# One hybrid decoder step on one core: scaled tokens transposed, vector rows in the token pool, stored decode rows written from SBUF

## The chip, the cores and the metric

The kernel runs on one core of one Trainium2 chip. The metric is the device time of one execution in microseconds. Engines are named PE (TensorE, matrix products), DVE (VectorE), ACT (ScalarE), POOL (GpSimd) and SP (SyncE, which issues most DMAs).

## The reference, cut to what matters

Two layers, each a token mixer and a squared-ReLU MLP. The first mixer is a causal Conformer convolution, the second RWKV-7 time mixing. There is one prompt of 1024 tokens with 16 learned meta tokens ahead of it, and eight decode sequences with one new token each.

```python
def _rmsnorm(x, g):
    y = xf * lax.rsqrt(jnp.mean(xf * xf, axis=-1, keepdims=True) + RMS_EPS)
    return (y * g).astype(x.dtype)

def _conformer_conv(h, buf, w_pw1, b_pw1, w_dw, b_dw, ln_g, ln_b, w_pw2, b_pw2):
    u = h @ w_pw1 + b_pw1
    u = u[..., :D_MODEL] * jax.nn.sigmoid(u[..., D_MODEL:])
    full = jnp.concatenate([buf, u], axis=1)             # buf: 30 stored rows of a sequence
    c = lax.conv_general_dilated(full, w_dw[:, None, :], ...)   # 31 taps, one filter per channel
    ...                                                  # LayerNorm over the channels -> cn
    out = jax.nn.silu(cn) @ w_pw2 + b_pw2
    return out, full[:, -CONV_BUF:]                      # the new 30 rows

for i in range(DEPTH):                                   # DEPTH = 2, D_MODEL = 1024, D_FF = 4096
    hn = _rmsnorm(h, norm_mix[i])
    out, ... = conformer_conv(hn, ...) if i == 0 else rwkv7(hn, ...)
    h = h + out
    h = h + square(relu(_rmsnorm(h, norm_mlp[i]) @ w_mlp_in[i])) @ w_mlp_out[i]
```

All data is float32. For a decode sequence the new conv state is its stored rows 1 to 29 and the new row; `conv_sample` (8, 30, 1024) is an output, and so are the prompt's last 30 rows, the RWKV states and the final norm of the tokens.

## The kernel before, in words

**Dense products.** The 1048 tokens are worked in three groups of 352, 348 and 348 columns (G0; the eight decode tokens are the last columns of group 2). Activations lie with the channel on the partition, so the tokens are transposed once, at the start. Each float32 operand is split into a high and a low part, and a product is the sum of three matmuls (`mm3`, L187 to L189): high by high, low weight by high, high weight by low. One weight tile is 1024 x 128 (512 KB), 24 matmuls. SP loads it into a slot of the pool "raw" (`load_raw`, L146; five slots), ACT casts the high part (L157), POOL subtracts the low part (L162), and both stand in a ring of slots until PE has used them.

**Who orders the work.** The program is written as generators: the main line (dense products) calls `fill()`, which lets a background generator go on for some points. On top of that the framework simulates a timeline and gives each engine its own fixed order of instructions; an engine carries out its list in that order and waits by semaphores, so an instruction that waits holds up all that stands behind it on its engine. DMA issues stand in these lists too. The issues of SP and ACT go round over eight completion counters, and a counter's next user waits until its last one has landed.

**The beginning** (`transpose_x`, `load_x`, `load_vecs`, `load_dw`). For each group, up to 128 tokens at a time land in `xt` (L414). ACT squares and sums them (L417; the squares go to a throwaway tile `xj`), takes the root (L418), DVE inverts it (L419): this is the factor of the RMS norm, in `ss[:, 2:3]`. PE transposes the raw tokens into `tx` (L450) for the residual. For the normed tokens DVE builds the diagonal matrix `dg` of the factors (L462) and PE multiplies `xt` with it (`tn`, L466): this transposes and scales in one float32 matmul. ACT (L468) and DVE (L469) then multiply by the norm's gain and split into `hn_h` and `hn_l`. Meanwhile `load_vecs` gathers the small vectors as rows of `stg` and transposes them, and `load_dw` does so with the convolution's 31 x 1024 weights (`wst`, L437; `ptw`, L440; `wdw`, L441). Both staging tiles are slots of the raw weight pool.

**The first mixer.** `pw1` makes `u` from the two halves of the first pointwise product (`pg`, `pa`; sigmoid at L481, product at L483). `conv` runs the 31 taps on DVE (L501, L504). The prompt's groups follow one another in the background of the dense products; `mean_parts` gathers the means of the LayerNorm (`acc_mu`, L223), which PE sums at L231.

**The decode rows.** `conv_states` writes the new rows (`cst`, `csd`; L545, L546). `conv_dec` loads the stored rows of eight sequences, in two tiles of 4 x 30 rows (`sdec`, L515), transposes them by channel block (`pw`, L521), copies them beside the new token's column (`win`, L523, L524) and sums the taps. `cst`, `csd` and the two `sdec` tiles share two slots. The stored rows 1 to 29 also go to the output `conv_sample`, by eight copies from DRAM to DRAM on ACT's queue (L1573). They stand late in the program's text, but have no input of the kernel's own to wait for, and the order puts them at 0.8 to 20.4 us.

After the first MLP comes the RWKV layer: its projections, 17 chunks of recurrence between them and the second MLP, the decode step and the final norm.

Of the kernel before, what the change touches and what calls it, by code (L numbers as in the profile page):

```python
# [8 lines left out]
F32 = mybir.dt.float32  # L9
F32R = mybir.dt.float32r  # L10
BF16 = mybir.dt.bfloat16
AF = mybir.ActivationFunctionType
ALU = mybir.AluOpType
# [3 lines left out]
P = 128  # L17
D = 1024
# [4 lines left out]
DEC = 8  # L23
NP_TOK = META + SEQ
T = NP_TOK + DEC
CW = 31
CB = CW - 1
# [21 lines left out]
def hybrid_step(tc, x_prompt, x_sample, state_conv, state_shift, state_wkv, meta_tokens,  # L49
# [8 lines left out]
    nc = tc.nc  # L58
    ctx = ExitStack()
    with ctx:  # L60
# [4 lines left out]
        ident = consts.tile([P, P], F32, name="ident")  # L65
# [3 lines left out]
        eps_t = consts.tile([P, 4], F32, name="eps_t")  # L69
        for i, e in enumerate((RMS_EPS, LN_EPS, GN_EPS)):  # L70
            nc.vector.memset(eps_t[:, i:i + 1], e)

        dram = pool(ctx, "dram", 1, space=bass.MemoryType.DRAM)
        d_x2 = dram.tile([P, KT, G0[2][1]], F32, name="d_x2")
# [47 lines left out]
        cur = {}  # L122
# [6 lines left out]
        def stat(name, tag, bufs, w=None):  # L129
            return cur["stat"].tile([P, w or cur["n"]], F32, name=name, tag=tag, bufs=bufs)  # L130
# [238 lines left out]
        with ExitStack() as l0:  # L369
# [36 lines left out]
                    out.append((c, w, parts))  # L406
                return out

            def load_x(pl, g):
                tiles = []  # L410
                for i, (c, w, parts) in enumerate(segments(g)):
                    xt = pl.tile([P, D], F32, name=f"xt{g}_{i}", tag="xt")
                    for r0, src in parts:
                        nc.sync.dma_start(xt[r0:r0 + src.shape[0], :], src)  # L414
                    junk = pl.tile([P, D], BF16, name=f"xj{g}_{i}", tag="xj", bufs=1)
                    ss = stat(f"ss{g}_{i}", "ss", 4, 4)
                    nc.scalar.activation(junk[:w, :], xt[:w, :], AF.Square, accum_out=ss[:w, 0:1])  # L417
                    nc.scalar.activation(ss[:w, 1:2], ss[:w, 0:1], AF.Sqrt, scale=1.0 / D, bias=eps_t[:w, 0:1])  # L418
                    nc.vector.reciprocal(ss[:w, 2:3], ss[:w, 1:2])  # L419
                    tiles.append((c, w, xt, ss))  # L420
                return tiles

            def load_vecs(tiles):

                for i in tiles:
                    st = cur["raw"].tile([P, D], F32, name=f"stg{i}", tag="raw")[:, :P]
                    nc.gpsimd.memset(st, 0.0)
                    for q, (name, ap) in enumerate(v for v in vecs if col[v[0]] // P == i):
                        r = col[name] % P
                        (nc.gpsimd if q % 2 else nc.scalar).dma_start(st[r:r + ap.shape[0], :], ap)  # L430
                    pt = bank("ptp")
                    nc.tensor.transpose(pt[:, :P], st, ident)
                    nc.vector.tensor_copy(pvec[:, i * P:(i + 1) * P], pt[:, :P])

            def load_dw():
                wst = cur["raw"].tile([P, D], F32, name="wst", tag="raw")[:CW, :]
                nc.scalar.dma_start(wst, conv_w_dw.rearrange("l w c -> (l w) c"))  # L437
                pt = bank("ptw")
                for k in range(KT):
                    nc.tensor.transpose(pt[:, k * CW:(k + 1) * CW], wst[:, k * P:(k + 1) * P], ident[:CW, :CW])  # L440
                nc.vector.tensor_copy(wdw, pt[:, :KT * CW].rearrange("p (k w) -> p k w", k=KT))  # L441

            def transpose_x(g, ah, al):
                n = G0[g][1]
                tiles = load_x(xin, g)
                yield 4
                for k in range(KT):
                    ps = bank(f"tx{g}_{k}")
                    for c, w, xt, ss in tiles:
                        nc.tensor.transpose(ps[:, c:c + w], xt[:w, k * P:(k + 1) * P], ident[:w, :w])  # L450
                    if g < 2:
                        (nc.scalar.copy if g else nc.vector.tensor_copy)(h[g][:, k, :n], ps[:, :n])
                    else:
                        t = tt(f"xs{k}", "t1")
                        nc.scalar.copy(t[:, :n], ps[:, :n])
                        nc.sync.dma_start(d_x2[:, k, :], t[:, :n])
                    yield 1
                if g == 0:
                    load_vecs([0])
                dg = stat(f"dg{g}", "acc0", 1)  # L460
                for c, w, xt, ss in tiles:
                    nc.vector.tensor_scalar(dg[:w, c:c + w], ident[:w, :w], ss[:w, 2:3], None, op0=ALU.mult)  # L462
                for k in range(KT):
                    ps = bank(f"tn{g}_{k}")
                    for c, w, xt, ss in tiles:
                        nc.tensor.matmul(ps[:, c:c + w], xt[:w, k * P:(k + 1) * P], dg[:w, c:c + w], start=True, stop=True)  # L466
                    gk = vec("norm_mix", k)
                    nc.scalar.activation(ah[:, k, :n], ps[:, :n], AF.Copy, scale=gk)  # L468
                    nc.vector.scalar_tensor_tensor(al[:, k, :n], ps[:, :n], gk, ah[:, k, :n].bitcast(F32),  # L469
                                                   op0=ALU.mult, op1=ALU.subtract)  # L470
                    yield 1
# [39 lines left out]
            def conv_dec(c, c_col):  # L511

                sd = [decp.tile([P, D], F32, name=f"sdec{i}", tag="st", bufs=2)[:4 * CB, :] for i in range(2)]
                for i in range(2):
                    nc.sync.dma_start(sd[i], state_conv[0, 4 * i:4 * i + 4].rearrange("b w d -> (b w) d"))  # L515
                yield 1
                for m in range(KT):
                    win = decp.tile([P, DEC, CW], F32, name=f"win{m}", tag="win")
                    ps = bank(f"pw{m}", "x")
                    for i in range(2):  # L520
                        nc.tensor.transpose(ps[:, i * 4 * CB:(i + 1) * 4 * CB], sd[i][:, m * P:(m + 1) * P],  # L521
                                            ident[:4 * CB, :4 * CB])
                    nc.scalar.copy(win[:, :, :CB], ps[:, :DEC * CB].rearrange("p (b w) -> p b w", b=DEC))  # L523
                    nc.gpsimd.tensor_copy(win[:, :, CB:CW], udec[:, m, :].unsqueeze(2))  # L524
                    nc.vector.tensor_mul(win, win, wdw[:, m:m + 1, :].broadcast_to([P, DEC, CW]))
                    rd = decp.tile([P, DEC], F32, name=f"rd{m}", tag="rd")
                    nc.vector.tensor_reduce(rd, win, axis=AX.X, op=ALU.add)
                    nc.scalar.activation(c[:, m, c_col:c_col + DEC], rd, AF.Identity, bias=vec("b_dw", m))
                    yield 1
# [935 lines left out]
        with ExitStack() as l1:  # L1465
# [103 lines left out]
            mixer_out(1, residp2, actp, fill, add)  # L1569
            for _ in rest:  # L1570
                pass
            for q in range(DEC):
                nc.scalar.dma_start(o_conv_sample[0, q, 0:CB - 1, :], state_conv[0, q, 1:CB, :])  # L1573
            g1 = group(1, actp, hidp, sums)
            fill, rest = filler(2 * KT + MLP2_POINTS, ([ranked(FN, final(0))], FB))
            add, sums = sums_of(2)
# [43 lines left out]
```

## Time and profile before

| what | value |
|---|---|
| runs | 2867.08, 2878.38 and 9711.41 us; median 2878.38 |
| profiled execution, time | 2870.67 us |
| its span in the profile | 2869.0 us |
| granted PE clock | 0.961 |
| busy share of PE, DVE, ACT, POOL | 94%, 68%, 47%, 59% |
| DMA traffic | 428.34 MB, 149 GB/s over the span |

A busy share is an average over stages with different limits, so the profile is read stage by stage: windows give the busy time of each engine in a stretch, and the timeline lists instructions with their start, length, engine and line, and in brackets the idle time before them and what ended it. Times are from the span's start. One of the three runs took more than three times as long as the others; the median is taken as it stands.

### The profile page before, as it was taken

To read this page: it belongs to the slowest core of one execution; us is meant where nothing else is said; L and a number is where in the kernel's file an instruction comes from. 1 tells how busy PE (TensorE), PEld (TensorE's weight loads), DVE (VectorE), ACT (ScalarE), POOL (GpSimd) and SP (SyncE) were. 2 spreads that over 40 slices of the span, in tenths; PEclk is the share of its full clock that TensorE was granted. 3 is DMA by queue.
4 is the path that set the end of the run, shared out by engine and by line. 5 is a ranking of instruction groups with operands and counts; after the bars stand their busy time and mean duration, and the time that the engine had idled before them with its cause. 6 is when DMAs were issued, how large, how long until landed. Compare 5 with 4: busy or idle time off the path is not lost. (4 is left out here: it accounts for less than half of the span.)

```text
span 2869.0 us, 54486 instructions
## 1 busy us (share of the span) xinstructions
PE 2690.9 (94%) x20554; PEld 2567.2 (89%) x20554; DVE 1962.3 (68%) x3794; ACT 1350.6 (47%) x2515; POOL 1703.3 (59%) x2295
## 2 busy tenths in 40 slices
PE   8999999999999898878799889889999999999998
PEld 8998999999999898867678788778889999999998
DVE  5999999995455546377986885689656764443444
ACT  5545444544354334464666766634445552222223
POOL 6677877887788775444433463656438783433432
PEclk9999999999999999888999999989989999999999
DMA  6662544454444542676788877766556742222211
GB/s 176 178 187 88 155 134 133 138 177 136 140 130 142 175 140 89 201 208 178 200 210 217 236 188 184 204 175 161 134 150 206 205 136 85 67 74 67 67 60 41
DMA packets 659285, 428.34 MB, mean 149 GB/s; under 512 B 126840, under 2 KB 609208, under 8 KB 659022
## 3 DMA queue, kind: packets, MB, share of 16 engines
q1 hardware_dynamic: 652780, 421.93, 52.4%
q10 hardware_dynamic: 6018, 2.89, 0.4%
q8 instruction: 162, 2.65, 0.4%
q14 instruction: 101, 0.83, 0.1%
q0 software_dynamic: 224, 0.03, 0.0%
HBM read 353.03 MB, written 72.66 MB: 148 GB/s over the span
## 5 line engine op out<-in xcount | busy, mean ns | idle before, releaser
L162 POOL TENSOR_TENSOR wo_lo<-wo_raw,wo_hi 128x256 fp32r<-128x256 f32 x736 | 564.1, 800 | 281.8 <-ACT wo_hi L157 269.0
L162 POOL TENSOR_TENSOR wi_lo<-wi_raw,wi_hi 128x256 fp32r<-128x256 f32 x640 | 491.5, 800 | 278.4 <-ACT wi_hi L157 266.3
L187 PE MATMUL out<-hh,wo_hi 128*128 128x352 f32 (+2 forms) x1536 | 504.0, 328 | 20.1 <-DVE h L340 10.9
L340 DVE TENSOR_TENSOR h<-h,out 128x352 f32<-128x352 f32 (+2 forms) x768 | 385.8, 509 | 196.8 <-PE out L189 196.2
L187 PE MATMUL ps_in<-m_h,wi_hi 128*128 128x352 f32 (+2 forms) x1536 | 498.3, 325 | 10.3 <-ACT m_h L269 8.3
L188 PE MATMUL out<-hh,wo_lo 128*128 128x352 f32 (+2 forms) x1536 | 499.5, 325 | 0.0
L189 PE MATMUL out<-hl,wo_hi 128*128 128x352 f32 (+2 forms) x1536 | 495.5, 325 | 4.2 <-DVE hl L141 4.2
L188 PE MATMUL ps_in<-m_h,wi_lo 128*128 128x352 f32 (+2 forms) x1536 | 497.2, 324 | 0.0
L189 PE MATMUL ps_in<-m_l,wi_hi 128*128 128x352 f32 (+2 forms) x1536 | 496.2, 323 | 0.0
L504 DVE SCALAR_TENSOR_TENSOR cv<-u,wdw,cv 128x352 f32<-128x352 f32 (+2 forms) x720 | 376.5, 572 | 0.7
L157 ACT CAST wi_hi<-wi_raw 128x1024 fp32r<-128x1024 f32 x160 | 168.1, 1050 | 392.9 <-PE out L189 187.6
L157 ACT CAST wo_hi<-wo_raw 128x1024 fp32r<-128x1024 f32 x184 | 192.9, 1049 | 313.8 <-PE out L189 146.6
L187 PEld LDWEIGHTS out<-hh,wo_hi 128*128 128x128 f32 x1536 | 292.8, 191 | 27.5 <-DVE h L340 14.8
L187 PEld LDWEIGHTS ps_in<-m_h,wi_hi 128*128 128x128 f32 x1536 | 290.6, 189 | 13.6 <-ACT m_h L269 8.4
L189 PEld LDWEIGHTS out<-hl,wo_hi 128*128 128x128 f32 x1536 | 291.9, 191 | 6.5 <-DVE hl L141 5.5
L188 PEld LDWEIGHTS out<-hh,wo_lo 128*128 128x128 f32 x1536 | 292.8, 191 | 1.6
L188 PEld LDWEIGHTS ps_in<-m_h,wi_lo 128*128 128x128 f32 x1536 | 290.7, 189 | 2.0
L189 PEld LDWEIGHTS ps_in<-m_l,wi_hi 128*128 128x128 f32 x1536 | 290.2, 189 | 1.5
L327 DVE SCALAR_TENSOR_TENSOR r<-ps_in,rs_m 128x352 f32<-128x352 f32 (+2 forms) x192 | 98.6, 515 | 234.1 <-PE ps_in L189 230.5
L141 DVE TENSOR_TENSOR hl<-s,hh 128x352 fp32r<-128x352 f32 (+2 forms) x192 | 144.4, 753 | 111.8 <-ACT hh L140 111.6
L329 ACT ACTIVATE s<-r 128x352 f32<-128x352 f32 (+2 forms) x192 | 93.8, 490 | 134.6 <-DVE r L327 134.4
L162 POOL TENSOR_TENSOR wv_lo<-wv_raw,wv_hi 128x256 fp32r<-128x256 f32 x96 | 79.9, 864 | 25.9 <-ACT wv_hi L157 25.6
(403 smaller groups left out, 6195.0 us busy)
## 6 DMA issues: line engine op xcount, KB each, us to landing
wi_raw<-in_w_mlp_in_dram SPq DMA_DIRECT2D x160, 512.0 KB, 4.1
wo_raw<-in_w_mlp_out_dram SPq DMA_DIRECT2D x160, 512.0 KB, 3.7
wr_raw<-in_rwkv_w_r_dram SPq DMA_DIRECT2D x32, 512.0 KB, 6.0
wk_raw<-in_rwkv_w_k_dram SPq DMA_DIRECT2D x32, 512.0 KB, 5.6
wv_raw<-in_rwkv_w_v_dram SPq DMA_DIRECT2D x32, 512.0 KB, 5.4
d_ab<-ab SPq DMA_DIRECT2D x32, 512.0 KB, 3.3
pg_raw<-in_conv_w_pw_dram SPq DMA_DIRECT2D x24, 512.0 KB, 5.1
pa_raw<-in_conv_w_pw_dram SPq DMA_DIRECT2D x24, 512.0 KB, 4.5
```

Of the source, the lines that this page charges most:

```text
L141: eng_lo.tensor_sub(lo, src, hi.bitcast(F32))
L157: nc.scalar.copy(hi[:, :a * b], raw[:, :a * b])
L162: eng_lo.tensor_sub(lo[:, cs], raw[:, cs], hi[:, cs].bitcast(F32))
L187: nc.tensor.matmul(ps, w[0], act[0], start=first, stop=False)
L188: nc.tensor.matmul(ps, w[1], act[0], start=False, stop=False)
L189: nc.tensor.matmul(ps, w[0], act[1], start=False, stop=last)
L327: nc.vector.scalar_tensor_tensor(r[:, :n], ps[:, :n], 0.0, rs[:, :n], op0=ALU.max, op1=ALU.mult)
L329: nc.scalar.activation(s[:, :n], r[:, :n], AF.Square)
L340: nc.vector.tensor_add(hv[:, 4 * i + m, :], hv[:, 4 * i + m, :], ps[:, :n])
L504: nc.vector.scalar_tensor_tensor(acc[m][:, :n], ug[:, m, j:j + n], wdw[:, m, j:j + 1], acc[m][:, :n], op0=ALU.mult, op1=ALU.add)
```

## The change

Four edits, all shown here:

1. The Square's output is kept as a float32 tile (`xn`), which is then overwritten with the scaled tokens (`xt` times the factor; DVE in group 0, ACT in groups 1 and 2). PE transposes it with the identity, in place of the product with a diagonal. The diagonal is gone.
2. One activation with Sqrt stands at the start, on the constants, so that the table of functions is loaded there.
3. `stg` and `wst` are tiles of the token pool `xin`: `stg` has a slot of its own, `wst` is one more user of the three slots of `xn`. The raw pool's five slots hold weights alone.
4. The eight copies from DRAM to DRAM on ACT's queue are gone. In `conv_dec` SP writes rows 1 to 29 of each sequence from the loaded tiles in SBUF.

```diff
         for i, e in enumerate((RMS_EPS, LN_EPS, GN_EPS)):
             nc.vector.memset(eps_t[:, i:i + 1], e)
+
+        nc.scalar.activation(eps_t[:, 3:4], eps_t[:, 0:1], AF.Sqrt)
...
-            def load_x(pl, g):
+            def load_x(pl, g, xns):
...
-                    junk = pl.tile([P, D], BF16, name=f"xj{g}_{i}", tag="xj", bufs=1)
+                    junk = pl.tile([P, D], F32, name=f"xn{g}_{i}", tag="xn")
+                    xns.append(junk)
...
-                    st = cur["raw"].tile([P, D], F32, name=f"stg{i}", tag="raw")[:, :P]
+                    st = xin.tile([P, P], F32, name=f"stg{i}", tag="stg", bufs=1)
...
-                wst = cur["raw"].tile([P, D], F32, name="wst", tag="raw")[:CW, :]
+                wst = xin.tile([P, D], F32, name="wst", tag="xn")[:CW, :]
                 nc.scalar.dma_start(wst, conv_w_dw.rearrange("l w c -> (l w) c"))
...
-                tiles = load_x(xin, g)
+                xns = []
+                tiles = load_x(xin, g, xns)
+                scaled = []
+                for i, (c, w, xt, ss) in enumerate(tiles):
+                    xs = xns[i]
+                    if g:
+                        nc.scalar.activation(xs[:w, :], xt[:w, :], AF.Copy, scale=ss[:w, 2:3])
+                    else:
+                        nc.vector.tensor_scalar(xs[:w, :], xt[:w, :], ss[:w, 2:3], None, op0=ALU.mult)
+                    scaled.append(xs)
                 yield 4
...
-                dg = stat(f"dg{g}", "acc0", 1)
-                for c, w, xt, ss in tiles:
-                    nc.vector.tensor_scalar(dg[:w, c:c + w], ident[:w, :w], ss[:w, 2:3], None, op0=ALU.mult)
                 for k in range(KT):
                     ps = bank(f"tn{g}_{k}")
-                    for c, w, xt, ss in tiles:
-                        nc.tensor.matmul(ps[:, c:c + w], xt[:w, k * P:(k + 1) * P], dg[:w, c:c + w], start=True, stop=True)
+                    for (c, w, xt, ss), xs in zip(tiles, scaled):
+                        nc.tensor.transpose(ps[:, c:c + w], xs[:w, k * P:(k + 1) * P], ident[:w, :w])
...
                 for i in range(2):
                     nc.sync.dma_start(sd[i], state_conv[0, 4 * i:4 * i + 4].rearrange("b w d -> (b w) d"))
                 yield 1
+                for i in range(2):
+                    for q in range(4):
+                        nc.sync.dma_start(o_conv_sample[0, 4 * i + q, 0:CB - 1, :], sd[i][q * CB + 1:(q + 1) * CB, :])
+                    yield 0
...
-            for q in range(DEC):
-                nc.scalar.dma_start(o_conv_sample[0, q, 0:CB - 1, :], state_conv[0, q, 1:CB, :])
```

## The prediction

> **What bounds the kernel now.** I read the page first, for the engine that fills the span and for the chain of waits that ended last.
>
> ```profile
> span 2869.0 us, 54486 instructions
> PE 2690.9 (94%) x20554; PEld 2567.2 (89%) x20554; DVE 1962.3 (68%) x3794; ACT 1350.6 (47%) x2515; POOL 1703.3 (59%) x2295
> PE   8999999999999898878799889889999999999998
> ## 4 chain that ended last, share of the span: by engine, by line
> PE 27%; POOL 5%; DVE 5%; issue 3%; DMA 2%; ACT 1%; SPq 0%; DVEq 0%; POOLq 0%; ACTq 0%
> ```
>
> TensorE (PE) is busy for 2690.9 of 2869.0 us, which leaves 178 us of idle time in all: a faster helper engine can give back no more than a share of that, while a wait that reaches PE costs its full length. So I looked next at the stretches the change touches, by windows: the beginning, the first mixer's dense products, and the stretch from 300 us on, where the stored decode rows are loaded.
>
> ```profile
> 0.00:70.00 70.00, 57.76 (x349) 55.74 (x350) 37.42 (x86) 37.92 (x58) 42.10 (x73) 0.95 0.64 179
> 60.00:204.00 144.00, 144.00 (x948) 143.77 (x947) 135.71 (x275) 72.97 (x122) 107.47 (x166) 1.00 0.63 175
> 320.00:370.00 50.00, 50.00 (x319) 49.91 (x317) 49.11 (x106) 22.90 (x38) 39.38 (x58) 1.00 0.44 134
> 370.00:490.00 120.00, 120.00 (x745) 119.56 (x745) 114.50 (x239) 49.65 (x72) 91.10 (x126) 1.00 0.44 134
> ```
>
> The columns after the length are busy us of PE, weight loads, VectorE (DVE), ScalarE (ACT) and GpSimd (POOL), then clock, DMA share and GB/s. In the first 70 us PE stands still for 12.2. From 60 to 204 and from 320 to 490 it never stops, and DVE is nearly full beside it: a microsecond taken off PE's work there is earned, and a stall put in there is not won back in that stretch.
>
> **Part 1 and 3, the beginning of group 0.** The timelines of ACT and PE, and the DMA view in slices of 1.25 us, show what the first dense product waits for.
>
> ```profile
> 6.19 0.28 ACTq L437 DMA_DIRECT2D wst<-in_conv_w_dw_dram  x1
> 18.66 1.04 ACT L157 CAST pa_hi<-pa_raw 128x1024 fp32r<-128x1024 f32 x1 [5.69 <-DMA pa_raw<-in_conv_w_pw_dram]
> 21.36 2.33 ACT L468 ACTIVATE hn_h<-tn,pvec 128x352 fp32r<-128x352 f32 x5
> ```
> ```profile
> 22.58 4.16 PE L466 MATMUL tn<-dg,xt 128*128 128x128 f32 x18 [4.67 <-DVE hn_l L469]
> 26.67 0.68 PE L440 MATMUL ptw<-ident,wst 31*128 31x31 f32 x8
> 27.28 0.43 PE L187 MATMUL ps_g<-hn_h,pg_hi 128*128 128x352 f32 x1
> 27.55 0.32 PE L188 MATMUL ps_g<-hn_h,pg_lo 128*128 128x352 f32 x1
> 27.71 0.32 PE L189 MATMUL ps_g<-hn_l,pg_hi 128*128 128x352 f32 x1
> ```
> ```profile
> GB/s 0 130 290 280 376 231 264 253 341 357 359 64 22 25 147 291 192 70 322 138 0 98 282 170 306 289 162 152 264 133 114 274 200 260 317 217 18 4 168 260
> wst<-in_conv_w_dw_dram ACTq DMA_DIRECT2D x1, 124.0 KB
> ```
>
> ACT stood 5.69 us behind the cast of pa_0, whose weights came late, and only then wrote hn_h, on which the last 18 passes of tn wait (4.67). At 15 to 17.5 us the DMA moves 22 and 25 GB/s. What moves there are the rows of wst: 4096 bytes at 25 GB/s are 0.164 us a row, one row after another, with the other engines empty. So 31 rows of 4 KB, an odd shape that divides into nothing, go over one DMA engine: 31 x 0.164 to 0.186 (at 22 GB/s) is 5.1 to 5.8 us.
>
> In the changed order wst is not issued at the start. Its tile now takes the slot of the first scaled-token tile, so its issue stands on ACT behind hn_h number 6 and waits for the last tn of group 0. ptw, which reads wst, stands in PE's order ahead of all dense products, as before. What is gained before that: the five raw slots all hold weights, the casts of pg_0, pa_0, pg_1, pa_1 come early, hn_h starts at 21.36 - 5.69 + 1.04 = 16.7 (the wait gone, one more cast ahead), and tn_7 ends near 20, allowing 3 us for its 18 cheaper passes. xt of the next group shares wst's completion counter, so its issue comes at about 21.3; one small transfer takes 1.7 us from issue to landing (the first figure of the row below), and the 31 rows 5.5 to 7 more with other loads beside them: wst lands near 29.8, ptw follows for 0.7, and the dense products start at about 30.8 instead of 27.28. That is +3.5 on PE: the gain of the casts is spent on a new wait behind ptw.
>
> ```profile
> DMA to landing us min/median/max: 1.7/2.6/3.6
> ```
>
> Against it stand the cheaper transposes in groups 1 and 2, in the window where PE is full. tn passes (fp32 product with a diagonal) and tx passes (plain transposes), each line with its count:
>
> ```profile
> L466 PE MATMUL tn<-dg,xt 128*128 128x128 f32 (+1 forms) x96 | 12.8, 269 | 0.0
> L450 PE MATMUL tx<-ident,xt 128*128 128x128 f32 (+1 forms) x30 | 4.6, 262 | 0.0
> ```
>
> 96 passes take 12.8 us, 30 transposes 4.6, so 0.153 each; the 48 transposes that replace the 96 passes take 7.4. That gives back 5.4 us, and PE alone stands at 3.5 - 5.4 = -1.9.
>
> The other candidate for the end of this stretch is DVE's convolution, which starts with u:
>
> ```profile
> 37.90 1.06 ACT L417 ACTIVATE xj<-xt 92x1024 bf16<-92x1024 f32 x1 [3.46 <-DMA xt<-in_x_prompt_dram]
> 42.56 0.16 DVE L419 RECIPROCAL ss<-ss 92x1 f32<-92x1 f32 x1 [7.59 <-ACT ss L418]
> 42.94 0.57 DVE L483 SCALAR_TENSOR_TENSOR u<-ps_a,pvec,sg 128x352 f32<-128x352 f32 x1
> 200.94 10.43 DVE L223 TENSOR_TENSOR acc_mu<-acc_mu,u 128x352 f32<-128x352 f32 x1
> 211.43 1.54 PE L231 MATMUL st_mu<-acc_mu,ones_d 128*128 128x352 f32 x2 [5.90 <-DVE acc_mu L223]
> ```
>
> u waits behind the reciprocal of a late token tile. In the changed order it stands behind the same reciprocal, but that one is no longer late (its tile's Square waits for ptw, whose slot it takes, and is through by about 33), so u follows the dense products: 24 matmuls at 0.16 (27.55 to 27.71) are 3.8 us, two tiles 7.6, so u at 30.8 + 7.6 = 38.4, 4.5 earlier. At 211 PE waits 5.90 for DVE's acc_mu, so DVE's gain counts there too. Between -1.9 (PE decides) and -4.5 (DVE decides) I take **-3**. The ends for the range: -5.4 if wst is early enough to cost nothing, +3.5 if the transposes' gain is lost in the wait for acc_mu. The extra scaling passes (ACT, 1.06 us for a tile by the Square's row) lie under the dense products; without that cover, three a group would be 3.2. The one table load moved to the start is hidden under the first token load; what it saves later is in u's time. I cost the different order inside the pointwise products and the recurrence, where a block of chunks stands 110 to 150 PE instructions later before both orders meet again, at nothing; a rival prices it.
>
> **Part 4, the stored rows.** Removed: eight DRAM-to-DRAM copies on ACT's queue, in the first 20 us. Added: eight writes of 29 x 1024 on SP's queue, in conv_dec. SP's changed order is: first load of sdec, wi_8, csd's write, writes 1 to 3, second load of sdec, wi_9, writes 4 to 8, then wo_3_0, wo_3_1. Before, the place looks like this:
>
> ```profile
> 306.00 0.36 SPq L515 DMA_DIRECT2D sdec<-in_state_conv_dram  x1
> 311.65 0.33 SPq L515 DMA_DIRECT2D sdec<-in_state_conv_dram  x1
> sdec<-in_state_conv_dram SPq DMA_DIRECT2D x2, 480.0 KB, 4.5
> 319.86 0.37 PE L521 MATMUL pw<-ident,sdec 120*128 120x120 f32 x2
> 335.89 1.05 ACT L157 CAST wo_hi<-wo_raw 128x1024 fp32r<-128x1024 f32 x1 [1.35 <-PE out L189]
> 336.84 0.35 ACT L523 COPY win<-pw 128x240 f32<-128x240 f32 x1
> 339.72 0.37 PE L521 MATMUL pw<-ident,sdec 120*128 120x120 f32 x2
> ```
>
> 29 rows divide no better than wst's 31, so each write is 29 rows on one engine. The copies are all of one shape, so whatever chooses the engine from the shape chooses alike; I take them to share one engine, which also carries its share of every weight tile. 232 rows stand in line there. Price of a row: 0.164 (25 GB/s) at the low end; at the high end what a crowded load shows, sdec's 4.5 us less 1.7, over the 8 rows that each of 15 engines gets, 0.35. I take 0.19, beside wst's slower slice, because one engine's rows are the same kind of traffic.
>
> The Trainium skill, "DMA: Bandwidth & Descriptors", section "Why a DMA increments its semaphore by 16 and not by 1", says that a queue of SP or ACT spreads a copy over the largest number up to 16 that divides the slowest dimensions of both sides, and uses the lowest-numbered engines. By it 29 and 31 rows give one engine, and always the same one. wst's 22 and 25 GB/s agree with the first half; no row here shows which engine successive copies take. By this rule the sum is the one below, by turns of engines it would be rival A's.
>
> First wait: the first load lands at 306.00 + 4.5 = 310.5, the first row of write 1 moves at 312.2 (1.7 later). Three writes, 87 x 0.19 = 16.5, then the second load's 8 rows, 1.5: it lands at 330.2. pw wants it at 319.86, so PE stands 10.3 us. Write 5 and the loads behind it wait on SP for the second load too.
>
> Second wait: writes 4 to 8 stand ahead of wo_3_0 and wo_3_1. The engine's line is 232 x 0.19 = 44.1, the 1.5, and its shares of wi_9, wo_3_0 and wo_3_1, 32 KB each at 25 GB/s, 1.3 each: wo_3_1 lands at 312.2 + 44.1 + 1.5 + 3.9 = 361.7. ACT casts wo_3_1 at 335.89 and only behind it copies win(2), and the fourth pw at 339.72 waits for that copy with 2.5 us to spare (339.72 - 336.84 - 0.35). So all above 335.89 + 2.5 = 338.4 reaches PE: 361.7 - 338.4 = **23.3 in all**, the 10.3 and 13 more. At 0.164 it is 17, at 0.35 it is 62. PE has no idle time after it to take it back. What the eight removed copies free, ACT's queue and the early DMA traffic, is contained in the earlier casts above.
>
> **Sum.** 2870.67 (the profiled execution, 1.7 over its span) - 3 + 23.3 = **2891 us**. The profiled run lies between the two undisturbed of the runs shown, 2867.08 and 2878.38, 0.3% under the median, so a median after may stand some microseconds above the sum.
>
> **The rivals.**
> A. The writes go over different engines, by turns. Then sdec's second load is behind 29 rows at most, 312.2 + 5.5 + 1.5 = 319.2, before 319.86, and nothing stalls: 2870.67 - 3 = 2868, not slower. For it: nothing in the rows fixes the engine. Against: equal shapes.
> B. The first wait comes, the second doesn't, because ACT's cast of wo_3 turns out to have more lead than the win copies show, or the later writes are delayed until PE has passed: 2870.67 - 3 + 10.3 = 2878. For it: the DMA share of 0.44 leaves the other 15 engines idle half the time. Against: five writes of 29 rows stand before wo_3_0 in one order.
> C. The row takes 0.35 us as in crowded loads: 2870.67 - 3 + 62 = 2930, slower by just over 2% of the profiled execution (from some 0.345 us a row on). For it: sdec's 4.5 us. Against: wst's rows beside other loads.
> D. The chunks of the recurrence that stand some 130 instructions later leave their waits uncovered once: 130 x 0.16 = 21 on top, 2912. For it: PE already shows 7 and 8 tenths in the middle slices. Against: both orders meet again before the end.
> That the beginning doesn't start the dense products earlier, as one would expect of it, is in the forecast itself.
>
> **How the numbers follow.** Forecast 0.48 (own range 2882 to 2900), A 0.22, B 0.13, C 0.10, D 0.07. The range leaves out C and the tails: 2862 (A with -5.4, and a little run-to-run spread) to 2916 (D). Faster by over 2% would be under 2813 to 2821, which no case reaches; I leave 0.02. Slower by over 2%, about what a measurement of this kernel can tell from no change: C and the worst of D, 0.12. Within: 0.86.
>
> **What would show it.** Right: ptw and the first dense product near 31 us; tn in groups 1 and 2 at about 3.7 us each; the first u near 38; a PE gap of about 10 us before the first pw near 320, waiting for sdec, and another of about 13 some 20 to 40 us later with ACT waiting for wo_raw; GB/s near 25 in parts of that stretch. Wrong: dense products before 27 us, no gap at pw (rival A), one gap alone (B), gaps of over 50 us together (C), or a loss that sits after 1600 us (D).

## The result and the profile after

| | before | after |
|---|---|---|
| median of 12 runs each | 2871.52 us | 2881.97 us |
| lowest run | 2865.03 us | 2877.08 us |
| span of the profiled execution | 2869.0 us | 2881.6 us |

The changed kernel is slower by 0.35%: the ratio of its runs to those of the kernel before is 1.0035, 95% interval [1.0023, 1.0046]. That is inside the 2%, and 2881.97 lies inside the whole range of 2862 to 2916, at the lower edge of the forecast's own 2882 to 2900. The forecast was 2891, a loss of 20 us, and the measured loss is 10. Disturbed runs (two of the kernel before took 3274.66 and 9711.41 us) are not in the ratio.

The page and the windows of the changed kernel, for the lines shown of before:

```profile
span 2881.6 us, 54361 instructions
PE 2672.5 (93%) x20482; PEld 2550.4 (89%) x20482; DVE 1958.0 (68%) x3788; ACT 1351.1 (47%) x2519; POOL 1701.4 (59%) x2295
PE   6999799999999899877799799979999999999998
```
```profile
0.00:70.00 70.00, 47.70 (x270) 44.90 (x271) 35.56 (x76) 34.46 (x55) 39.84 (x67) 0.83 0.61 165
60.00:204.00 144.00, 139.85 (x890) 138.75 (x889) 134.76 (x262) 72.60 (x124) 104.56 (x160) 0.98 0.61 172
320.00:370.00 50.00, 35.94 (x197) 35.19 (x198) 28.54 (x63) 12.88 (x23) 21.74 (x34) 0.80 0.34 110
370.00:490.00 120.00, 120.00 (x754) 119.52 (x753) 116.22 (x243) 50.27 (x74) 93.63 (x130) 1.00 0.46 136
```

PE has 18 us less work and the span is 12.6 longer, so some 31 us of idle time are new. Two windows hold most of them: the first 70 us (47.70 busy against 57.76) and 320 to 370 (35.94 against 50.00). The first is the wait for wst:

```profile
20.57 0.23 ACTq L440 DMA_DIRECT2D wst<-in_conv_w_dw_dram  x1
33.09 1.03 PE L443 MATMUL ptw<-ident,wst 31*128 31x31 f32 x8 [12.77 <-DMA wst<-in_conv_w_dw_dram]
44.73 0.58 DVE L492 SCALAR_TENSOR_TENSOR u<-ps_a,pvec,sg 128x352 f32<-128x352 f32 x1 [8.91 <-PE ps_a L191]
```

wst is issued at 20.57, behind hn_h, and PE stands 12.77 us before ptw. The second, in the timelines of SP, PE and ACT and the DMA view of 300 to 350 in slices of 1.25 us, is the line of stored rows:

```profile
310.21 1.00 SPq L528 DMA_DIRECT2D out_dram<-sdec  x3
312.01 0.34 SPq L524 DMA_DIRECT2D sdec<-in_state_conv_dram  x1
312.40 1.75 SPq L148 DMA_DIRECT2D wi_raw<-in_w_mlp_in_dram  x1
314.20 19.40 SPq L528 DMA_DIRECT2D out_dram<-sdec  x5
333.71 7.02 SPq L148 DMA_DIRECT2D wo_raw<-in_w_mlp_out_dram  x2
```
```profile
327.82 0.46 PE L534 MATMUL pw<-ident,sdec 120*128 120x120 f32 x1 [10.95 <-DMA sdec<-in_state_conv_dram]
353.21 1.04 ACT L159 CAST wo_hi<-wo_raw 128x1024 fp32r<-128x1024 f32 x1 [11.66 <-DMA wo_raw<-in_w_mlp_out_dram]
356.42 0.66 PE L534 MATMUL pw<-ident,sdec 120*128 120x120 f32 x2 [6.23 <-ACT win L536]
GB/s 144 0 216 282 20 69 302 199 272 16 121 270 175 261 62 29 26 26 26 26 26 25 22 32 29 26 26 26 26 26 26 203 241 234 211 125 315 46 85 319
```

For most of 20 us (318.75 to 338.75) the DMA moves 26 GB/s, one row of 4096 bytes in 0.158 us, with almost nothing beside it. PE waits 10.95 us for the second load of sdec; ACT waits 11.66 for wo_3_0, and only then copies win(2), for which PE waits again. SP itself is held too: the issues of writes 4 to 8 take 19.40 us, since they wait for earlier landings, and the loads of wo_3 are issued at 333.71 instead of 316.75.

How the delay grows is read by one kind of event that every trace has, ACT's cast of a weight tile: the k-th cast of the same tile, its start in one trace less its start in the trace of before. The table holds this for the changed kernel and for the experiments told below, in us. Each column is one execution.

| cast of (start before) | after | split4 | undo4 | only4 | tr_only | acc_pool | best_split | best_all |
|---|---|---|---|---|---|---|---|---|
| pg, 21st (182.2) | +10.3 | +8.7 | +11.0 | +2.4 | +0.7 | -1.0 | -2.0 | -8.2 |
| p, 1st (226.1) | -2.1 | -3.6 | -1.3 | +2.3 | -11.6 | -10.8 | -14.4 | -20.6 |
| wi, 7th (308.7) | -3.7 | -4.6 | -2.5 | +1.1 | -12.5 | -8.3 | -15.7 | -24.6 |
| wo, 7th (332.0) | +21.2 | -3.6 | -2.0 | +23.3 | -12.1 | -8.3 | -15.3 | -24.4 |
| wo, 35th (590.3) | +16.3 | -5.4 | -5.2 | +20.3 | -15.6 | -7.8 | -19.4 | -25.0 |
| wo, 91st (1074.7) | +15.4 | -6.6 | -6.6 | +19.4 | -17.9 | -11.0 | -21.2 | -25.9 |
| wo, 127th (2207.5) | +13.3 | -5.9 | +3.2 | +12.0 | -22.0 | -19.4 | -32.3 | -30.8 |
| wo, last (2813.1) | +12.7 | -5.9 | +3.1 | +11.4 | -21.9 | -19.7 | -33.2 | -31.1 |

In the column "after" three things stand out. At 182 us the kernel is 10 us behind, and between 182 and 226 this turns into a gain of 2. The decode rows cost 24.9 by this cast (from -3.7 to +21.2). Afterwards some 8 us come back.

### The profile page after: what moved, and what is told of

Same layout as the page of the kernel before. It is cut to its first block, busy times and chain, and to the rows that moved or that the text cites. A ratio compares the mean times of both kernels' runs of the same rounds, so it can differ in the third digit from the quotient of the medians.

```text
span 2881.6 us, 54361 instructions
## 1 busy us (share of the span) xinstructions
PE 2672.5 (93%) x20482; PEld 2550.4 (89%) x20482; DVE 1958.0 (68%) x3788; ACT 1351.1 (47%) x2519; POOL 1701.4 (59%) x2295
## 4 chain that ended last, share of the span: by engine, by line
PE 29%; DVE 7%; POOL 6%; DMA 4%; issue 4%; ACT 1%; SPq 1%; DVEq 0%; POOLq 0%; ACTq 0%
PE ps_in L191 3%; PE ps_in L189 3%; PE ps_in L190 3%; POOL wo_lo L164 3%; PE out L189 3%; PE out L191 3%; PE out L190 3%; POOL wi_lo L164 2%; PE A L1219 1%; DMA bk<-d_ab 1%; DVE ni L1179 1%; DVE tt L1178 1%; POOL wv_lo L164 1%; PE ps_oo L189 0%; PE Y L1320 0%
## 5 line engine op out<-in xcount | busy, mean ns | idle before, releaser
L164 POOL TENSOR_TENSOR wv_lo<-wv_raw,wv_hi 128x256 fp32r<-128x256 f32 x96 | 81.8, 881 | 32.7 <-ACT wv_hi L159 25.7
```

The lines of the kernel that those rows point to most:

```text
L164: eng_lo.tensor_sub(lo[:, cs], raw[:, cs], hi[:, cs].bitcast(F32))
```

## The experiments

All ratios are to runs of the kernel before on the same chip.

**undo4.** Part 4 alone is undone.

```diff
-                for i in range(2):
-                    for q in range(4):
-                        nc.sync.dma_start(o_conv_sample[0, 4 * i + q, 0:CB - 1, :], sd[i][q * CB + 1:(q + 1) * CB, :])
-                    yield 0
...
+            for q in range(DEC):
+                nc.scalar.dma_start(o_conv_sample[0, q, 0:CB - 1, :], state_conv[0, q, 1:CB, :])
```

> The changed kernel with part 4 alone undone: the stored rows go by eight copies from DRAM to DRAM on ACT's queue again. Theory (one DMA engine's line of 232 rows stalls PE at the decode rows): the gap before pw (10.95 us after the change) and ACT's wait for wo_raw (11.66) are gone, PE stands at 370 us some 22 us earlier than in the changed kernel. For the end there are two readings of the 9 us that the changed kernel gives back after 330 us. If later waits swallow a delay, little of the 22 is seen at the end beyond what the beginning brought before 300 us (-3): about 2868. If the order of the later work is what gave it back, it is given back here too: about 2860. Rival (the rows don't matter, the loss is elsewhere): 2882, as the changed kernel.

Measured: 2878.22 us, ratio 1.0018 [1.0005, 1.003]. Neither 2868 nor 2860; the end alone lies nearer the rival's 2882. But the local part held: no gap at pw, and at the seventh wo cast the kernel stands at -2.0 instead of +21.2. It then loses 10 us between 1075 and 2207, in the recurrence. Its order of instructions there is not that of the changed kernel (in the traces 1023 of PE's 20,482 matmuls stand at other positions, some 900 of them between 1908 and 2185 us), so its end compares two schedules and not one edit.

**only4.** The kernel before with part 4 alone.

```diff
                 yield 1
+                for i in range(2):
+                    for q in range(4):
+                        nc.sync.dma_start(o_conv_sample[0, 4 * i + q, 0:CB - 1, :], sd[i][q * CB + 1:(q + 1) * CB, :])
+                    yield 0
...
-            for q in range(DEC):
-                nc.scalar.dma_start(o_conv_sample[0, q, 0:CB - 1, :], state_conv[0, q, 1:CB, :])
```

> The kernel before with part 4 alone: only the writes from SBUF are new. In its order one write stands ahead of the second load of the stored rows, seven behind it and all eight ahead of wo_3. Theory of one engine and one line: a short first gap (0 to 2 us, 29 rows at 0.16 after the first load), and nearly all of the 22 us in the second wait, on wo_raw; GB/s near 26 for some 35 us. At the end about 2872 + 22 = 2894 if nothing is given back, 2882 to 2886 if later waits swallow part of a delay. Rival (the beginning's new wait for wst is what costs): 2872, as before.

Measured: 2883.28 us, ratio 1.0032 [1.0021, 1.0044]. As one line predicts, the first gap is absent, because one write instead of three stands ahead of the second load, and the second takes nearly all:

```profile
320.97 0.37 PE L525 MATMUL pw<-ident,sdec 120*128 120x120 f32 x2
355.32 1.04 ACT L157 CAST wo_hi<-wo_raw 128x1024 fp32r<-128x1024 f32 x1 [17.06 <-DMA wo_raw<-in_w_mlp_out_dram]
358.54 0.66 PE L525 MATMUL pw<-ident,sdec 120*128 120x120 f32 x2 [12.40 <-ACT win L527]
```

The delay goes from +1.1 to +23.3. So at this place part 4 costs the same 22 to 25 us with and without the other parts. The end, 10 us behind, keeps half of it: up to 1448 us PE has exactly the order of the kernel before, and its matmuls are 21.8 us late at 360 and 23.1 at 1440; then the order of the recurrence departs, and 11 us come back.

**split4.** The changed kernel with each write cut in two.

```diff
-                        nc.sync.dma_start(o_conv_sample[0, 4 * i + q, 0:CB - 1, :], sd[i][q * CB + 1:(q + 1) * CB, :])
+                        for a, b in ((0, 16), (16, CB - 1)):
+                            nc.sync.dma_start(o_conv_sample[0, 4 * i + q, a:b, :], sd[i][q * CB + 1 + a:q * CB + 1 + b, :])
```

> The changed kernel with each write of 29 rows cut into one of 16 and one of 13 rows, sixteen writes in all; the same bytes on the same queue at the same place. Theory (the count of rows decides over how many engines a copy goes): the 26 GB/s stretch goes, each engine has about 16 rows in all, 3 to 5 us; no gap before pw, none at wo_raw: the time of the kernel with part 4 undone, within 3 us. Rival (it is the eight issues and their waits on SP, not the engine): sixteen issues make the gaps longer, about 2890.

Measured: 2858.95 us, ratio 0.9946 [0.9925, 0.9966]. This is the cleanest of the comparisons: the computing instructions of PE, DVE, ACT and POOL stand in exactly the order of the changed kernel, and SP has eight issues more. From 320 to 370 PE is full again, and pw waits for nothing:

```profile
320.00:370.00 50.00, 50.00 (x317) 49.92 (x316) 49.83 (x109) 22.40 (x37) 39.63 (x59) 1.00 0.52 150
315.74 0.37 PE L535 MATMUL pw<-ident,sdec 120*128 120x120 f32 x2
```

Same bytes, same queue, the same stretch, more issues: 23 us less (2881.97 - 2858.95; 25 by the two ratios). The count of rows in one write, 29, is what cost them. SP's order is not quite the same: three pieces (45 rows) instead of three writes (87 rows) stand ahead of the second load, and a load of wo_3 stands ahead of the last five pieces. That alone would not empty the line, since all 232 rows at one row in 0.155 us are 36 us, and here the rows have left by 322, many at once. The expected end, within 3 us of undo4, was missed by 19: the two stand 1.6 us apart at 332 and part in the recurrence.

**actq4.** The eight writes on ACT's queue.

```diff
-                        nc.sync.dma_start(o_conv_sample[0, 4 * i + q, 0:CB - 1, :], sd[i][q * CB + 1:(q + 1) * CB, :])
+                        nc.scalar.dma_start(o_conv_sample[0, 4 * i + q, 0:CB - 1, :], sd[i][q * CB + 1:(q + 1) * CB, :])
```

> The changed kernel with the eight writes of 29 rows issued on ACT's queue instead of SP's. They still go over one engine, for some 37 us, but the weights no longer stand behind them in the same queue. Theory A (the line is the queue's: whatever stands behind a write in its own queue waits, another queue takes turns): both gaps shrink to under 4 us each, about 2865 to 2870. Theory B (the line is the engine's: every weight tile's share on it waits until the rows are through): both gaps stay above 8 us, about 2882.

Measured: 2878.08 us, ratio 1.0015 [1.0002, 1.0027]; neither theory as written. The loss at the decode rows is 22 us, but by a third way:

```profile
317.22 0.32 PE L534 MATMUL pw<-ident,sdec 120*128 120x120 f32 x1 [2.16 <-DMA sdec<-in_state_conv_dram]
317.25 16.63 ACTq L528 DMA_DIRECT2D out_dram<-sdec  x4
333.98 1.04 ACT L159 CAST wo_hi<-wo_raw 128x1024 fp32r<-128x1024 f32 x1 [20.27 <-issue]
337.86 0.66 PE L189 MATMUL out<-hh,wo_hi 128*128 128x352 f32 x1 [15.88 <-DVE h L342]
```

The first gap shrinks to 2.16 us, as A said: from another queue the writes no longer stand ahead of the second load. But ACT's last four issues take 16.63 us, waiting for earlier landings, and its casts stand behind them. The line was moved to an engine that has work of its own.

**wst_early.** wst lands at the start, in a corner of u[2].

```diff
-                wst = xin.tile([P, D], F32, name="wst", tag="xn")[:CW, :]
-                nc.scalar.dma_start(wst, conv_w_dw.rearrange("l w c -> (l w) c"))
+                wst = u[2][:CW, 0:4, :2 * P]
+                nc.scalar.dma_start(wst, conv_w_dw.rearrange("l w (k c) -> (l w) k c", k=4))
...
```

> The changed kernel with one thing other: wst, the convolution's 31 rows, lands in a corner of u[2], which nobody uses yet, instead of the slot of xn_0, so its load waits for nothing and is issued at the start. Everything else, the eight writes of 29 rows too, stays. In the changed kernel ptw waited 12.77 us for it and the dense products started at 34.1. Theory: ptw follows tn at once, dense products start near 21.5, u (44.7) near 32, and most of the 12.6 us is still there at 300 us, since PE is full in between: 8 to 12 us off the end, 2870 to 2874. Rival (the end of that stretch is set by DVE's convolution and the wait at acc_mu, which had slack): under 3 us, 2880.

Measured: 2875.44 us, ratio 1.0012 [0.9998, 1.0026]: 6.5 us better than the changed kernel, less than the 8 to 12 expected, and ptw is not at 21 but at 28.77. The reason is in ACT's timeline and the DMA view of the first 50 us:

```profile
15.34 0.29 ACT L421 ACTIVATE ss<-ss,eps_t 128x1 f32<-128x1 f32 x1 [5.91 <-DMA stg<-in_norm_mix_dram]
28.77 1.06 PE L443 MATMUL ptw<-ident,u 31*128 31x31 f32 x8
GB/s 0 53 239 297 333 210 47 28 25 25 23 11 39 224 335 290 291 290 291 295 363 413 332 286 253 196 242 192 86 132 314 207 279 41 0 7 7 0 68 326
```

Issued first, the 31 rows (here in pieces of 1024 bytes) are still moving from 8.75 to 13.75 us, at 23 to 28 GB/s. Rows of stg land behind them, ACT waits for those, and the whole start is later.

**wst_split.** wst in the changed kernel's slot and place, cut in two.

```diff
-                nc.scalar.dma_start(wst, conv_w_dw.rearrange("l w c -> (l w) c"))
+                for a, b in ((0, 16), (16, CW)):
+                    nc.scalar.dma_start(wst[a:b, :], conv_w_dw[0, a:b, :])
```

> The changed kernel with wst's late load cut into 16 and 15 rows, in the same slot and at the same late place. It separates the two things that make wst late, its issue at 20.6 and its one engine. If the engine is most of it, it lands near 25 instead of 32.9 and the dense products start near 26: 6 to 8 us earlier at 70 us. If the late issue and the other loads on the queue are most of it, near 31. The end moves by what wst_early shows to be worth, less its part: 2874 to 2882.

Measured: 2875.2 us, ratio 1.0006 [0.9992, 1.0019]; ptw at 28.96, between the two readings, after a wait of 8.69 us instead of 12.77. The one engine was a third of the wait; the rest is left to the late issue and the loads ahead of it.

**best_split.** Both cures in the changed kernel: wst in u[2] from the start in two pieces of 16 and 15 rows, and the writes of split4.

```diff
+                wst = u[2][:CW, 0:4, :2 * P]
+                for a, b in ((0, 16), (16, CW)):
+                    nc.scalar.dma_start(wst[a:b], conv_w_dw[0, a:b, :].rearrange("w (k c) -> w k c", k=4))
...
+                        for a, b in ((0, 16), (16, CB - 1)):
+                            nc.sync.dma_start(o_conv_sample[0, 4 * i + q, a:b, :], sd[i][q * CB + 1 + a:q * CB + 1 + b, :])
...
```

> The changed kernel with both cures: wst early in a corner of u[2] and cut into 16 and 15 rows, and each write of 29 rows cut into 16 and 13. With the cut writes alone the median was 2859. If the early wst gives 8 to 12 us of its own, 2847 to 2851; if the stretch to 300 us has slack, 2857 to 2860.

Measured: 2837.37 us, ratio 0.9878 [0.9857, 0.9898]. ptw is at 21.20, without a wait. This beats the kernel before by 34 us, and the better of the two readings, 2847, by 10. The table shows where: 15 us are gained by 332, and 11 of the others come between 1075 and 2207, in the recurrence, for which no edit was tried.

**tr_only.** The kernel before with part 1 alone (the hunks of load_x and transpose_x).

```diff
-                        nc.tensor.matmul(ps[:, c:c + w], xt[:w, k * P:(k + 1) * P], dg[:w, c:c + w], start=True, stop=True)
+                        nc.tensor.transpose(ps[:, c:c + w], xs[:w, k * P:(k + 1) * P], ident[:w, :w])
...
```

> The kernel before with part 1 alone: the tokens are scaled first and transposed with the identity; table set, stg, wst and the stored rows as before. By the sum: tn in groups 1 and 2 takes 3.7 us each in place of 6.4, the dense products start near 26 in place of 27.3, and 5 to 7 us are gained by 300 us: 2866 to 2868. Rival (PE waits for acc_mu at 211 anyway): 2871 to 2873.

Measured: 2847.32 us, ratio 0.9915 [0.9896, 0.9933]: 24 us, where 5 to 7 were expected. The terms of the sum are there: tn takes 3.69 us in each of groups 1 and 2, the products start at 25.7, and by PE's matmuls into ps_a, compared one by one, the kernel is 5.1 us ahead at 165 us. Between 165 and 178 it loses 5.7, which is told below. The rest comes between 182 and 226 us (from +0.7 to -11.6 in the table) and later. The windows of 204 to 230, of before, of the changed kernel and of this one:

```profile
204.00:230.00 26.00, 17.99 (x92) 16.14 (x92) 26.00 (x40) 8.87 (x15) 15.03 (x21) 0.83 0.33 98
```
```profile
204.00:230.00 26.00, 26.00 (x163) 25.57 (x162) 25.50 (x53) 12.33 (x19) 21.00 (x29) 1.00 0.43 126
```
```profile
204.00:230.00 26.00, 26.00 (x159) 25.14 (x159) 25.09 (x52) 12.70 (x18) 22.92 (x31) 1.00 0.46 136
```

In the kernel before PE was idle for 8.0 of these 26 us, and ran at a clock of 0.83 when it ran. In both others it is full, at 1.00. What is gone is the wait for acc_mu: DVE's add that began at 200.94 took 10.43 us, and ended when POOL's run of subtractions did. The last stretch of that run, in POOL's timeline of the kernel before, ends at 211.0; it began at 199.95 and had no pause:

```profile
199.95 2.83 POOL L162 TENSOR_TENSOR pa_lo<-pa_raw,pa_hi 128x256 fp32r<-128x256 f32 x4
...
208.24 2.76 POOL L162 TENSOR_TENSOR pg_lo<-pg_raw,pg_hi 128x256 fp32r<-128x256 f32 x4
```

In the changed kernel POOL pauses between tiles here, and the same add takes 0.82 us although POOL's next four subtractions have begun:

```profile
213.23 0.82 DVE L225 TENSOR_TENSOR acc_mu<-acc_mu,u 128x352 f32<-128x352 f32 x1 [0.22 <-ACT u L518]
```
```profile
212.93 3.10 POOL L164 TENSOR_TENSOR pa_lo<-pa_raw,pa_hi 128x256 fp32r<-128x256 f32 x4 [1.29 <-ACT pa_hi L159]
```

But the collision has moved rather than gone. In the changed kernel it is the add before this one that is caught, and it holds up hn_l, which stands behind it on DVE and for which PE waits:

```profile
171.86 5.84 DVE L225 TENSOR_TENSOR acc_mu<-acc_mu,u 128x352 f32<-128x352 f32 x1
174.53 2.79 POOL L164 TENSOR_TENSOR pg_lo<-pg_raw,pg_hi 128x256 fp32r<-128x256 f32 x4
177.63 0.57 DVE L478 SCALAR_TENSOR_TENSOR hn_l<-tn,pvec,hn_h 128x348 fp32r<-128x348 f32 x1
178.25 0.66 PE L191 MATMUL ps_g<-hn_l,pg_hi 128*128 128x348 f32 x1 [3.93 <-DVE hn_l L478]
```

In the kernel before that add took 0.53 us. tr_only has the same stall (an add of 5.82 us, a wait of 3.92), and best_split too (5.81 and 3.92).

**acc_pool.** Whether that add was the cause is tried in the kernel before, without any part of the change: the sums for the mean go to POOL alone.

```diff
-            for i, eng in enumerate((nc.gpsimd, nc.vector)):
+            for i, eng in enumerate((nc.gpsimd, nc.vector if square else nc.gpsimd)):
```

> The kernel before with one edit in mean_parts: the sums for the mean, acc_mu, are all added on POOL instead of half on DVE. In the kernel before, DVE's add at 200.94 took 10.43 us, as long as POOL ran its subtractions without a break, and PE waited 5.90 for it, then 2.1 more, at a clock of 0.72 to 0.93; from 204 to 230 PE was busy 17.99 of 26 us. In the changed kernel the same add took 0.82 and PE was busy for all 26. Theory (the gain of part 1 beyond its 5.4 us is this wait gone): without DVE's add the wait at st_mu shrinks below 3 us and the kernel is some 6 to 10 us ahead of before at 266 us, 2862 to 2866 at the end. Rival 1: POOL's own queue of subtractions delays its adds by as much, and st_mu waits for POOL instead: 2871, as before. Rival 2 (the wait is not what held the stretch): 2870.

Measured: 2850.95 us, ratio 0.9926 [0.9898, 0.9953]. The wait at st_mu is gone, PE is busy for 25.25 of the 26 us at clock 1.00, and the kernel is 10.8 ahead at 226, with diagonal products, late weights and all. The end is 24 us ahead by the medians and 21 by the ratio, more than expected; 8 us of it come in the recurrence (-11.0 to -19.4). So one add on DVE cost the kernel before some 10 us at this place, and an edit that keeps it from meeting POOL's run earns that here.

**tr_split.** The kernel before with part 1, split writes as in split4, and wst in the raw pool, split.

```diff
                 wst = cur["raw"].tile([P, D], F32, name="wst", tag="raw")[:CW, :]
+                for a, b in ((0, 16), (16, CW)):
+                    nc.scalar.dma_start(wst[a:b, :], conv_w_dw[0, a:b, :])
...
```

> The kernel before with part 1, wst in the raw pool as before but cut into 16 and 15 rows, and part 4 with each write cut into 16 and 13 rows; parts 2 and 3 left out. Part 1 alone was at 2847, both cures in the changed kernel at 2837. If parts 2 and 3 bring something of their own once wst is early, this ends behind 2837, at 2842 to 2847; if not, 2835 to 2840.

Measured: 2842.99 us, ratio 0.989 [0.9866, 0.9914], at the lower end of the first reading. By the ratios it is 3 us behind best_split, and the intervals of the two overlap, so what parts 2 and 3 bring is at most a few us, and not told apart from nothing.

**best_all.** best_split with the edit of acc_pool.

```diff
+            for i, eng in enumerate((nc.gpsimd, nc.vector if square else nc.gpsimd)):
```

> The changed kernel with both cures (wst early in u[2] and cut into 16 and 15 rows, writes cut into 16 and 13) and the sums of acc_mu on POOL alone. If moving acc_mu off DVE is worth something beside the wait at 200 us, it ends below 2837: 2828 to 2834. If the 24 us that the same edit brought to the kernel before were that wait and no more, 2835 to 2840, since the wait is already gone with the cures.

Measured: 2839.74 us, ratio 0.9872 [0.9848, 0.9896]: at the end the same as best_split, as the second reading has it. Its reason does not hold, though. At 165 us the two are level by PE's matmuls into ps_a (8.3 and 7.8 ahead); then best_split meets its add of 5.81 us and this kernel, which has no such add, runs on without a pause. The table has it 6.2 us further ahead at 182, 8.9 at 309 and 9.1 at 332. So the edit earns 6 to 9 us beside the cures, and they are lost again after 332, more than half of them between 1075 and 2207, in the recurrence.

## Why the prediction was right, and where its terms were off

**The stored rows: right, with some luck in the size.** One engine, all eight writes in its line, two waits. First wait 10.3 forecast, 10.95 measured; both together 23.3 forecast, 24.9 by the casts and 22.2 by PE's matmuls against those of split4 (0.9 late at 300 us, 23.1 at 370). split4 shows the cause by one edit.

The single packets in the trace show the line itself: 4096-byte rows one at a time from 316 until 327.40, then a share of wi_9, then 145 rows without a pause until 351.46, then a share of wo_3_0 until 352.74, whose cast starts at 353.21. A row came 0.155 us after the one before, below the forecast's lowest bound, and the forecast had wo_3_0 through only at 312.2 + 44.1 + 1.5 + 2 x 1.3 = 360.4. That the sum still came out is luck in part: the kernel was 3.7 us ahead when it met the line, the cast that waited was wo_3_0's (332.05 in the trace of before) and not wo_3_1's at 335.89, and PE ran slower after each wait. As plain idle time PE lost 17.2 us of the 60 from 310 to 370. SP's late issue of wo_3 cost nothing on this engine, which had no pause.

One line was read too widely: wst's last row begins at 15.73, so the slice of 25 GB/s from 16.25 us shows other transfers. The rows of wst lie 0.18 apart there, inside the bounds used. And one thing in the trace of before was passed over: the removed copies, of the same 29 rows but from DRAM to DRAM, went as 16 pieces of 7424 bytes each, the first one's all begun between 2.2 and 2.7 us. So what part 4 changed was not the queue alone but how far a copy spreads.

The rule named in the prediction (the Trainium skill, "DMA: Bandwidth & Descriptors", section "Why a DMA increments its semaphore by 16 and not by 1") has its second half borne out by this: had the first three writes gone over three engines, the second load would have been through by some 319 (rival A's sum), and it held PE until 327.82. Pieces of 16 and 13 rows left no such stretch.

Rival A (turns of engines) and rival C (0.35 us a row) are out by the same line, rival B by the two waits. Rival D's loss in the recurrence did not come in the changed kernel (+15.4 at 1075, +13.3 at 2207); undo4 had one of 9.8 us there.

**The beginning: the sum right by luck, two terms wrong.** At the seventh wi cast the changed kernel is 3.7 us ahead; -3 was forecast. But that is the sum of errors that cancel. The transposes of group 0 ended at 20.3, as forecast; wst was to land at 29.8, and ptw ran at 33.09, since the load took some 12 us from its issue and not 8.5, with the next group's tokens and weights in the same line. And after standing still PE was slow:

```profile
33.00:45.00 12.00, 11.91 (x60) 11.88 (x61) 0.84 (x3) 5.66 (x8) 2.61 (x4) 0.72 0.19 51
```

A clock of 0.72 over 12 us makes two tiles take 10 us, not 7.6. The first u, forecast at 38.4, came at 44.73, later than before. So the step "+3.5 on PE" was +9.3 by 50 us (PE's matmuls into ps_a, one by one). From there the transposes gave back 5.6 by 165 us, where 5.4 was forecast. The other wrong term is acc_mu. The prediction treated the 5.90 us as a bound to be shared by DVE and PE. It was a collision that a shift of the order moves: the changed kernel meets it earlier, with the add of 5.84 us, and loses 6.5 between 165 and 178; the one of the kernel before, worth 8.0 us of idle time and the slower clock behind it, is gone, which is the 12.4 between the first two rows of the table.

The two engines' collision fits what the Trainium skill, "SBUF — State Buffer", section "Who interferes with whom", says: a DVE instruction with two inputs in SBUF contends with a GpSimd instruction that reads SBUF, and the loser waits. The rows of 10.43 and 5.84 us agree, and show more: the adds outlasted some fourteen and eight subtractions of 0.7 us, not one, and each ended 0.4 us after POOL's run. The row of 0.82 us shows that it need not; what decides between the two stays open.

**The transposes: the size right.** 3.7 us a group forecast, 3.69 measured:

```profile
60.00:120.00 60.00, 3.69 (x24) 3.10 (x24) 4.63 (x8) 4.37 (x8) 1.00 0.47 135
```

**After 332 us: the term that made the loss half as large.** The prediction said that PE takes nothing back, and costed the later order at nothing. The first half nearly held. Against split4, which has the same order on all computing engines, PE's matmuls are 23.1 us late at 370, 21.7 at 590, 21.9 at 1900 and 18.7 at the end, and the medians differ by 23.0; only4 keeps its delay up to 1440 us. So with the order unchanged nearly all of the rows' cost is still there at the end.

The second half failed. The -3.7 at 309 us and the 22.2 of the decode rows make 18.5, and the changed kernel ended 12.7 behind in the profiled execution and 10.4 by the medians: 6 to 8 us were gained later. split4, the same order without the rows' cost, was 4.6 ahead at 309 us and 14.0 at the end by the medians, 5.9 in its profiled execution, the slowest of its six. In another order the same stretch can cost: from 1075 to 2207, the recurrence, the columns of the table move by -11 to +10. So the term that was off is the order, put at nothing. What in the order makes a good or a bad draw was not tried, and stays open; nor is one profiled execution a measure for it, since runs of one kernel spread over some 10 us.

## What to carry to other kernels

Look at the row count of every DMA before its bytes: 29 rows of 4 KB took 23 us more than 16 + 13 rows, because one engine carried them all and the loads behind them in that queue waited. Moving the odd transfers to another engine's queue only moved the wait here, since the issues wait for landings too. And when a small edit gains or loses more than its sum, look for a wait in the old trace that was an accident of the order; it may be worth curing by itself. Then look whether the wait is gone in the new trace or stands at another place.

## What the runs showed of the hardware that was not expected

One DVE add of 352 columns, 0.82 us at one place of the changed kernel, took 10.43 us in the kernel before while POOL ran without a pause, and 5.84 us at another place of the changed kernel; both ended when POOL's run ended. After 12.77 us of standing still PE's matmuls came 0.29 us apart until 39.8 us and 0.16 after that, with a granted clock of 0.72 over 33 to 45 us, so a wait can cost more than its length. Eight writes of 29 rows from SBUF went one row at a time, 0.155 us each, while copies of the same rows from DRAM to DRAM went in 16 pieces at once. A load of 31 rows issued first held up the small loads behind it on its own queue, and gained 6.5 us over the same load issued 20 us later, where 8 to 12 were expected; cut in two and still late, it gained as much.
